# Branch hints, gates in the one-hot rows, and a reordered end in a one-core attention and mixture-of-experts kernel

## Chip, cores and metric

The kernel runs on one core of a Trainium2 chip, as one program in one launch. The metric is the device time in microseconds (us); a kernel's time is the median of its runs.

## What is computed

The reference is two blocks over 256 tokens of width 1024, batch 1. The first is a sparse attention mixer; the second has two layers, each with an attention and convolution mixer, a feed-forward part and a gated side input. The change touches only the end of the last layer: the mixture of 8 experts of which each token uses 2, and the gate behind it.

```python
top_vals, top_idx = lax.top_k(logits, TOP_K)            # TOP_K = 2 of 8 experts
gates = jax.nn.softmax(top_vals, axis=-1)
for e in range(N_EXPERTS):
    out = out + combine[:, e:e + 1] * swiglu(xt, w1[e], w3[e], w2[e])
h = h + out
gate = jax.nn.sigmoid(rmsnorm(h, ple_norm_g[i]) @ ple_gate_w[i])
h = h + gate * (p[i] @ ple_proj_w[i])
```

## The kernel before

All is float32. Tokens stand as two tiles of 128 rows (`NT = 2`, index `t`). The weights, 491 MB of DMA traffic in all, are streamed by SyncE (SP) in pieces of 512 KB into a ring of buffers; a piece's buffer is filled again once its last reader is done. All engines run their instructions in the order in which the code is written (`manual_schedule`).

Experts are run in steps (`STEPS`) of one expert and one chunk of its hidden width, two experts alternating. Only the tokens of an expert are gathered, by a one-hot matrix of token against place in the expert's list: the first 64 places (`SET`) always, the places from 65 to 96 and from 97 to 128 (two times `SUB`) only if the expert has so many tokens. A step has three weight products, each through `wide` (line 1475): w1 and w3 (`up`) and w2 (`down`). `wide` issues the product of the first 64 places and puts off `rest`, a branch on TensorE alone (`If(many() > SET)`, line 1496, with one for over 96 inside, line 1499), which is issued by `catch_up` after the next product's first weight part. There are 98 such outer branches: 96 from 32 steps of three products, and 2 from `result_logits`. Where the count is at most 64, TensorE jumps over the instructions of the rare products.

When an expert is finished, `way_back` (line 1424) builds the one-hot rows `oh2` from positions and the 0/1 selection (`where`, line 1408), TensorE turns them round (`turn`) into `back`, and `scatter` (line 1575) multiplies `back` by the expert's results `ys` into PSUM and adds that to the residual `h`, weighted with the gate, by VectorE's scalar_tensor_tensor (line 1596). `scatter` is called per token tile, in two pieces that lie between other products, with a branch of its own (line 1602).

At the end the last gate matrix (`gate_w`) is multiplied with the expert results directly: `result_T` turns the last expert's results round and `result_logits` (line 1655) multiplies them with `gate_w` into `zs`, which is scattered like `ys`, but into `logit`. The end of `experts` (line 1767 on) is: last `down`, scatter of `ys` into `h` for both tiles with one branch (line 1781), `result_logits`, square sums of `h` on ScalarE (`halves`, line 451) and the root on VectorE (`rstd`), scatter of `zs` into `logit`, and per quarter (one tile, 512 columns) sigmoid on ScalarE (line 1799), product with `value` and sum with `h` on VectorE (lines 1800, 1801) and the store.

Of the kernel before, what the change touches and what calls it, by code (L numbers as in the profile page):

```python
# [19 lines left out]
P = 128  # L20
D = 1024
S = 256
NT = 2
# [190 lines left out]
class _Net:  # L214
# [1190 lines left out]

    def where(self, pos, t, e):
        return pos[:, t, e : e + 1], self.sel[:, t, e : e + 1], ALU.is_equal, ALU.mult

    def places(self, sp, e, base=0):

# [11 lines left out]

    def way_back(self, sp, e, base=0):

        pos = self.based(sp, base)
        oh = self.t(sp, [P, NT, 3, P], "oh2")
        for t in range(NT):
            first = self.slots[:, 0:SET].unsqueeze(1).to_broadcast([P, 2, SET])  # L1430
            self.nc.vector.tensor_scalar(oh[:, t, 0].rearrange("p (d n) -> p d n", d=2), first, *self.where(pos, t, e))
            rest = self.slots[:, SET:CAP].rearrange("p (s n) -> p s n", s=2).unsqueeze(2).to_broadcast([P, 2, 4, SUB])
            self.nc.vector.tensor_scalar(oh[:, t, 1:3].rearrange("p s (d n) -> p s d n", d=4), rest, *self.where(pos, t, e))
# [12 lines left out]
        return back, turn  # L1446
# [29 lines left out]
    def wide(self, key, outs, lhs, n, many, take, mids=None):  # L1476

        mids, ws = mids or {}, self.ws
        parts = ws.take(key)
        end = parts[-1][1][1]

        def product(s, j, k0, k1):
            w = ws.get(j)
            d = 4 if s else 2
            r, m = P // d, 2 * n // d
            c = m if s == 2 else 0
            for k in range(k0, k1):  # L1490
# [81 lines left out]
    def results(self):  # L1572
        return self.t(self.act, [P, 2, 512], "xl", bufs=3)

    def scatter(self, t, e, back, ys, many=None, to=None, tag="tr"):


        ps = []
        to = self.h[:, t, :] if to is None else to[t]
        rows = [slice(SET * j, SET * j + SET) for j in range(2)]  # L1580

        def first():
            ps[:] = [self.bank(tag) for _ in range(2)]
            for j in range(2):
                self.mm(ps[j], back[rows[j], 0, t * P : t * P + P], ys[rows[j], 0, :], start=True, stop=True, skip_group_check=True)

        def others():
            for i in range(2):
                for d in range(2):
                    for j in range(2):  # L1590
                        self.mm(ps[j][:, d * 256 : d * 256 + 256], back[rows[j], 1 + 2 * i + d, t * P : t * P + P],
                                ys[rows[j], 1, i * 256 : i * 256 + 256], start=False, stop=i == 1, skip_group_check=True)

        def add(j):
            v = to[:, j * 512 : j * 512 + 512]
            self.nc.vector.scalar_tensor_tensor(v, ps[j], self.gates[:, t, e : e + 1], v, ALU.mult, ALU.add)  # L1596

        def second():
            if many is None:
                others()  # L1600
            else:
                with self.tc.If(many() > SET):  # L1602
                    others()
            for j in range(2):
                add(j)

        return first, second, others, add

# [77 lines left out]
    def experts(self, sp):  # L1686
# [23 lines left out]
        for i, (e, c) in enumerate(STEPS):  # L1710
# [14 lines left out]
            if done is not None:  # L1725
                back[done], turn = self.way_back(sp, done)
                mids.setdefault(6, []).append(turn)
                late = {2 + 2 * t + k: [f] for t in range(NT) for k, f in enumerate(self.scatter(t, done, back[done], ys[done], F(number, done))[:2])}
            if i == LAST + 2:
                for j, (t, k0) in enumerate((t, k0) for t in range(NT) for k0 in (0, 4)):  # L1730
                    mids.setdefault(3 + j, []).append(F(self.gate_inputs, t, k0))
# [13 lines left out]
                zs = self.t(self.act, [P, 2, 512], "x", bufs=3)  # L1745
            if i == LAST + 7:
                x = STEPS[LAST][0]
                late = {2 * t + k: [f] for t in range(NT) for k, f in enumerate(self.scatter(t, x, back[x], zs, F(number, x), self.logit)[:2])}
# [19 lines left out]
        turn()  # L1768
        self.catch_up()
        hidden(*prev)  # L1770
        finish(*prev[:2])
        self.result_T(ys[e], yT[1], 0)
        self.catch_up()
        self.result_T(ys[e], yT[1], 1)
        self.sets.pop("mm")

        def scattered(ys, to):
            steps = [self.scatter(t, e, back[e], ys, None, to, ("tr", "mm")[t]) for t in range(NT)]
            for f in steps:
                f[0]()  # L1780
            with self.tc.If(many() > SET):
                for f in steps:
                    f[2]()
            return [F(f[3], j) for f in steps for j in range(2)]

        for f in scattered(ys[e], None):
            f()
# [7 lines left out]
        for (t, j), f in zip(((t, j) for t in range(NT) for j in range(2)), scattered(zs, self.logit)):  # L1795
            f()
            c = slice(j * 512, j * 512 + 512)
            sg, hv = self.t(self.wp, [P, 1024], "wl", bufs=PARTS)[:, 0:512], self.h[:, t, c]
            nc.scalar.activation(sg, self.logit[t][:, c], AF.Sigmoid, scale=r[:, t : t + 1])  # L1799
            nc.vector.tensor_mul(sg, sg, self.value[t][:, c])  # L1800
            nc.vector.tensor_add(hv, hv, sg)  # L1801
            nc.sync.dma_start(self.out[:, t, c], hv)

    def overflow(self, sp, xT, ys):
# [4 lines left out]
        with self.tc.If(most > CAP):  # L1809
            self.ws = _Direct(self, self.stream)  # L1810
            for e in range(NE):
                oh = self.places(sp, e, CAP)
                for k in (0, 4):
                    self.gather(oh, xT, k)
                back, turn = self.way_back(sp, e, CAP)
                turn()
                for c in range(NC):
                    n = CHUNKS[c][1] // 2
                    self.up(("w1", e, c), xT, s, n, None, True)
                    self.up(("w3", e, c), xT, s, n, None, False)  # L1820
                    self.down(("w2", e, c), ys, self.hidden(sp, s, n), n, None, c == 0)
                for t in range(NT):
                    for f in self.scatter(t, e, back, ys)[:2]:
                        f()
            self.ws = self.stream

# [237 lines left out]
```

## Time and profile before

| | us |
|---|---|
| median of 3 runs | 1792.64 (1789.38 to 1797.64) |
| the profiled execution's own time | 1791.19 |
| its span, first to last instruction | 1789.0 |
| TensorE (PE) busy | 1670.9 (93%) |
| VectorE (DVE) busy | 670.6 (37%) |
| ScalarE (ACT) busy | 504.8 (28%) |
| GpSimd (POOL) busy | 144.0 (8%) |
| granted TensorE clock, mean | 0.977 |

The profile is of one execution. A row of the timeline names start and length in us, the engine, the line of the kernel, the operation, output and inputs by the program's names, shape, and how many equal instructions were merged; in brackets stands how long the engine was idle before and what released it. "PEq L1496" as a releaser is TensorE's instruction queue at that branch. PEld is TensorE's loading of weights, and a float32 product shows as two matrix instructions. The experts run from about 800 us on; the last weights land just before 1740 us, and what follows is the end.

### The profile page before, as it was taken

To read this page: it belongs to the slowest core of one execution; us is meant where nothing else is said; L and a number is where in the kernel's file an instruction comes from. 1 tells how busy PE (TensorE), PEld (TensorE's weight loads), DVE (VectorE), ACT (ScalarE), POOL (GpSimd) and SP (SyncE) were. 2 spreads that over 40 slices of the span, in tenths; PEclk is the share of its full clock that TensorE was granted. 3 is DMA by queue.
4 is the path that set the end of the run, shared out by engine and by line. 5 is a ranking of instruction groups with operands and counts; after the bars stand their busy time and mean duration, and the time that the engine had idled before them with its cause. 6 is when DMAs were issued, how large, how long until landed. Compare 5 with 4: busy or idle time off the path is not lost. (4 is left out here: it accounts for less than half of the span.)

```text
span 1789.0 us, 24489 instructions
## 1 busy us (share of the span) xinstructions
PE 1670.9 (93%) x9778; PEld 1001.4 (56%) x9781; DVE 670.6 (37%) x1131; ACT 504.8 (28%) x831; POOL 144.0 (8%) x146
## 2 busy tenths in 40 slices
PE   8999989999999989999997999999999989898984
PEld 6887768778888868873324434445333354233331
DVE  6656776585555586651111220011211113101214
ACT  5546645654444456631000000000000000010001
POOL 2002332510000022400000000000000000000000
PEclk9999999999999999999999999999999999999987
DMA  8654335445555558478999998999699998888960
GB/s 275 199 170 145 104 106 191 143 152 188 188 187 181 180 180 307 162 305 344 406 414 410 386 370 337 366 396 403 230 378 401 412 411 323 313 327 320 391 256 25
DMA packets 174777, 491.24 MB, mean 275 GB/s; under 512 B 16670, under 2 KB 21206, under 8 KB 174576
## 3 DMA queue, kind: packets, MB, share of 16 engines
q1 hardware_dynamic: 170224, 474.54, 70.8%
q0 software_dynamic: 4352, 13.74, 2.6%
q8 instruction: 160, 2.62, 0.6%
q14 instruction: 41, 0.34, 0.1%
HBM read 486.08 MB, written 2.14 MB: 273 GB/s over the span
## 5 line engine op out<-in xcount | busy, mean ns | idle before, releaser
L287 PE MATMUL mm<-wh,xh 128*128 128x512 f32 (+3 forms) x888 | 317.4, 433 | 13.1 <-PEq L1809 6.8
L335 DVE TENSOR_TENSOR wl<-raw,wh 128x1024 fp32r<-128x1024 f32 x206 | 260.8, 1276 | 129.6 <-ACT wh L331 120.0
L287 PE MATMUL mm<-wh,xl 128*128 128x512 f32 x680 | 271.2, 399 | 1.0 <-DVE xl L506 0.9
L331 ACT CAST wh<-raw 128x1024 fp32r<-128x1024 f32 x218 | 227.0, 1049 | 128.6 <-PE mm L287 66.6
L287 PE MATMUL mm<-wl,xh 128*128 128x512 f32 (+3 forms) x924 | 253.9, 425 | 2.3 <-PEq L1496 2.0
L1536 DVE TENSOR_TENSOR sw_s<-sw_s,s 128x512 f32<-128x512 f32 (+1 forms) x64 | 39.7, 620 | 414.1 <-PE s L287 377.4
L287 PE MATMUL mm<-raw,xh 128*64 128x512 f32 (+3 forms) x1340 | 185.8, 456 | 8.8 <-PEq L1496 6.7
L287 PE MATMUL o<-raw,sw_g 128*64 128x512 f32 (+1 forms) x1228 | 182.6, 496 | 10.8 <-PEq L1496 8.3
L287 PE MATMUL s<-raw,xh 128*64 128x512 f32 (+3 forms) x1344 | 176.9, 453 | 12.6 <-PEq L1496 9.8
L287 PEld LDWEIGHTS mm<-wh,xh 128*128 128x128 f32 (+2 forms) x888 | 141.2, 176 | 59.9 <-issue 19.2
L287 PEld LDWEIGHTS mm<-wl,xh 128*128 128x128 f32 (+2 forms) x924 | 141.0, 172 | 54.0 <-issue 14.2
L287 PEld LDWEIGHTS mm<-wh,xl 128*128 128x128 f32 x680 | 129.3, 190 | 28.9 <-DVE xl L506 2.6
L1548 ACT COPY sw_g<-tr 128x512 f32<-128x512 f32 (+1 forms) x32 | 17.0, 532 | 440.2 <-PE tr L290 409.9
L287 PEld LDWEIGHTS o<-raw,sw_g 128*64 128x64 f32 (+1 forms) x1228 | 68.4, 124 | 114.7 <-issue 91.9
L287 PEld LDWEIGHTS s<-raw,xh 128*64 128x64 f32 (+1 forms) x1344 | 69.2, 124 | 111.6 <-issue 76.8
L287 PEld LDWEIGHTS mm<-raw,xh 128*64 128x64 f32 (+1 forms) x1340 | 67.7, 125 | 97.3 <-issue 73.7
L1534 ACT ACTIVATE sw_s<-mm 128x512 f32<-128x512 f32 (+1 forms) x64 | 34.8, 544 | 195.7 <-PE mm L287 161.0
L1557 DVE TENSOR_TENSOR xl<-xl,o 128x512 f32<-128x512 f32 x48 | 32.9, 686 | 144.6 <-PE o L287 131.4
L287 PE MATMUL s<-wh,xh 128*64 128x512 f32 (+5 forms) x292 | 62.9, 493 | 5.2 <-PEq L1602 3.8
L287 PE MATMUL o<-wh,sw_g 128*128 128x512 f32 (+2 forms) x264 | 60.9, 478 | 3.5 <-DMA raw<-in_moe_w_dram 2.0
L333 POOL TENSOR_TENSOR wl<-raw,wh 128x1024 fp32r<-128x1024 f32 x12 | 30.3, 2554 | 324.4 <-ACT wh L331 304.4
L287 PE MATMUL o<-wl,sw_g 128*64 128x512 f32 (+2 forms) x224 | 51.9, 515 | 3.6 <-DMA wl<-in_moe_w_dram 1.5
(388 smaller groups left out, 1661.9 us busy)
## 6 DMA issues: line engine op xcount, KB each, us to landing
raw<-in_moe_w_dram SPq DMA_DIRECT2D x465, 512.0 KB, 9.9
wh<-in_moe_w_dram SPq DMA_DIRECT2D x100, 512.0 KB, 9.8
wl<-in_moe_w_dram SPq DMA_DIRECT2D x100, 512.0 KB, 10.0
raw<-in_dense_w_dram SPq DMA_DIRECT2D x84, 512.0 KB, 4.6
raw<-in_w_in_dram SPq DMA_DIRECT2D x48, 512.0 KB, 4.4
raw<-in_nsa_w_in_dram SPq DMA_DIRECT2D x44, 512.0 KB, 5.1
raw<-in_w_o_dram SPq DMA_DIRECT2D x16, 512.0 KB, 4.9
raw<-in_ple_gate_w_dram SPq DMA_DIRECT2D x16, 512.0 KB, 6.3
```

The costliest lines, as they stand in the source:

```text
L287: self.nc.tensor.matmul(out, lhsT, rhs, start=start, stop=stop, **kw)
L331: self.nc.scalar.copy(wh, v)
L333: self.nc.gpsimd.tensor_tensor(wl, v, wh.bitcast(F32), ALU.subtract)
L335: self.owed.append(lambda: self.nc.vector.tensor_sub(wl, v, wh.bitcast(F32)))
L1534: nc.scalar.activation(s[:, i, :n], ps[i][:, :n], AF.Silu)
L1536: nc.vector.tensor_mul(s[:, i, :n], s[:, i, :n], ps[i][:, :n])
L1548: copy(g[:, i, : n // P, :], ps[:, :n].rearrange("p (q n) -> p q n", n=P))
L1557: self.nc.vector.tensor_add(ys[:, i, :], ys[:, i, :], y[i])
```

## The change

1. Each outer branch of `wide` gets a label, and halfway through the parts of its product the code marks "LikelyTaken" for that label on TensorE.
2. `where` takes the values it multiplies with; `way_back` passes the gates in place of the 0/1 selection. So `back` holds the gate, and the sum in `scatter` becomes a plain tensor_add.
3. At the end, `logit` is copied into four PSUM banks by a product with the identity, ahead of the last `down`; the scatter of `zs` is added up on top of it there, and the sigmoid reads PSUM.
4. The scatter of `ys` into `h` is done per tile with a branch each; square sums and root stand ahead of `result_logits`. A sigmoid of one column loads ScalarE's table early.
5. Both copies of `result_logits` are on ScalarE. The four sigmoids are issued first, then the products on VectorE; two of the four sums with `h` are on GpSimd.

```diff
-    def where(self, pos, t, e):
-        return pos[:, t, e : e + 1], self.sel[:, t, e : e + 1], ALU.is_equal, ALU.mult
+    def where(self, pos, t, e, value=None):
+        return pos[:, t, e : e + 1], (self.sel if value is None else value)[:, t, e : e + 1], ALU.is_equal, ALU.mult
...
-            self.nc.vector.tensor_scalar(oh[:, t, 0].rearrange("p (d n) -> p d n", d=2), first, *self.where(pos, t, e))
+            self.nc.vector.tensor_scalar(oh[:, t, 0].rearrange("p (d n) -> p d n", d=2), first, *self.where(pos, t, e, self.gates))
...
+        self.n += 1
+        label = f"rare_{self.n}"
+
         def rest():
-            with self.tc.If(many() > SET):
+            with self.tc.If(many() > SET, label=label):
...
+            if i == len(parts) // 2 and many is not None:
+
+                self.tc.mark_branch_hint_location(label, "LikelyTaken", engines=(mybir.EngineType.PE,))
...
-            self.nc.vector.scalar_tensor_tensor(v, ps[j], self.gates[:, t, e : e + 1], v, ALU.mult, ALU.add)
...
+                self.nc.vector.tensor_add(v, v, ps[j])
...
+    def spread(self, ps, t, back, ys, start):
+        for j in range(2):
+            r = slice(SET * j, SET * j + SET)
+            self.mm(ps[j], back[r, 0, t * P : t * P + P], ys[r, 0, :], start=start, stop=True, skip_group_check=True)
...
         def take(i):
-            if i:
-                self.nc.vector.tensor_copy(zs[:, i, :], z[i])
-            else:
-                self.nc.scalar.copy(zs[:, i, :], z[i])
+            self.nc.scalar.copy(zs[:, i, :], z[i])
...
         hidden(*prev)
+        nc.scalar.activation(self.t(self.act, [P, 1], "warm"), self.gT[:, 0:1], AF.Sigmoid)
+
+        lg = []
+        for t, tag in zip(range(NT), ("mm", "s")):
+            self.sets.pop(tag)
+            lg.append([self.bank(tag) for _ in range(2)])
+            for j in range(2):
+                self.mm(lg[t][j], self.ident, self.logit[t][:, j * 512 : j * 512 + 512], start=True, stop=True)
         finish(*prev[:2])
...
-        self.result_logits(yT[1], zs, many)
+        for t in range(NT):
+            for f in self.scatter(t, back[e], ys[e], many):
+                f()
         sq = self.sq_tile(NT)
         junk = self.t(self.wp, [P, 1024], "wh", bufs=PARTS)
         for t in range(NT):
             self.halves(sq[:, t], t, junk)
         r = self.rstd(sq)
+        self.result_logits(yT[1], zs, many)
         self.catch_up()
...
+        for t in range(NT):
+            self.spread(lg[t], t, back[e], zs, False)
+        with self.tc.If(many() > SET):
+            for t in range(NT):
+                self.spread_rare(lg[t], t, back[e], zs)
...
+        for t, _, ps, sg in pieces:
+            nc.scalar.activation(sg, ps, AF.Sigmoid, scale=r[:, t : t + 1])
+        for i, (t, c, _, sg) in enumerate(pieces):
+            hv = self.h[:, t, c]
             nc.vector.tensor_mul(sg, sg, self.value[t][:, c])
-            nc.vector.tensor_add(hv, hv, sg)
+            (nc.vector if i > 1 else nc.gpsimd).tensor_tensor(hv, hv, sg, ALU.add)
             nc.sync.dma_start(self.out[:, t, c], hv)
```

The order of the instructions in the built program shows where these land. First the start of TensorE's program, in the change:

```order
L2059 UNCONDITIONAL_BRANCH
L2059 BRANCH_PREFETCH_HINT x98
L290 MATMUL tr_132<-c_ident_86,h_85 128x128 x4
L290 MATMUL s_137<-c_ident_86,x_89 128x8
L290 MATMUL tr_154<-c_ident_86,h_85 128x128 x4
```

Before, the first transposes follow the branch directly. All 98 hints stand here, ahead of the first work, in the reverse order of their branches; none stands in the products, where the code marks them.

Second, TensorE between the turning of the last hidden values (`sw_s`) and the last `down` (`o<-raw,sw_g`), in the change:

```order
L290 MATMUL tr_27053<-c_ident_86,sw_s_26641 128x128 x2
L287 MATMUL mm_27059<-x_24962,c_ident_86 128x512
L287 MATMUL mm_27060<-x_24962,c_ident_86 128x512
L287 MATMUL s_27063<-x_24963,c_ident_86 128x512
L287 MATMUL s_27064<-x_24963,c_ident_86 128x512
L287 MATMUL o_7225<-raw_26830,sw_g_27048 64x512 x2
L287 MATMUL o_7225<-raw_26832,sw_g_27048 64x512 x2
L287 MATMUL o_7225<-raw_26834,sw_g_27048 64x512 x2
L287 MATMUL o_7225<-raw_26836,sw_g_27048 64x512 x2
```

The four products with the identity (`c_ident`; the `x` tiles are `logit`) are new; before, the `down` follows the transposes at once.

Third, the last work of VectorE (`wl` holds the sigmoids, `raw` the `value` tiles), in the change:

```order
L1809 TENSOR_TENSOR wl_27281<-wl_27281,raw_14224 128x512
L1809 TENSOR_TENSOR wl_27282<-wl_27282,raw_14224 128x512
L1809 TENSOR_TENSOR wl_27283<-wl_27283,raw_14308 128x512
L1810 TENSOR_TENSOR h_85<-h_85,wl_27283 128x512
L1809 TENSOR_TENSOR wl_27284<-wl_27284,raw_14308 128x512
L1810 TENSOR_TENSOR h_85<-h_85,wl_27284 128x512
```

Before, 13 instructions stand there: a copy of `zs` and four times scatter's sum, product and sum. The sums of `wl_27281` and `wl_27282` with `h` are now GpSimd's last two instructions.

## Rows read from the trace of the kernel before

**Rows 1.** The page: busy time of the engines; DMA share in 40 slices.
```profile
PE 1670.9 (93%) x9778; PEld 1001.4 (56%) x9781; DVE 670.6 (37%) x1131; ACT 504.8 (28%) x831; POOL 144.0 (8%) x146
...
DMA  8654335445555558478999998999699998888960
```

**Rows 2.** Stretches of the experts: length, busy time by engine, clock, DMA share, GB/s.
```profile
800.00:1000.00 200.00, 177.89 (x896) 73.38 (x900) 26.93 (x55) 19.41 (x35) 0.00 (x0) 0.97 0.98 390
1000.00:1200.00 200.00, 197.70 (x1768) 82.76 (x1769) 28.57 (x45) 11.72 (x20) 0.00 (x0) 1.00 0.93 366
```

**Rows 3.** TensorE's waits at branches: us in total, times, longest.
```profile
PE o L287 <- PEq L1496: 12.7, 16, 3.0
PE s L287 <- PEq L1496: 11.5, 21, 5.4
PE mm L287 <- PEq L1496: 10.7, 12, 2.9
...
PE s L287 <- PEq L1602: 5.1, 12, 3.3
```

**Rows 4.** Instructions of TensorE's queue at lines 1496 and 1781: ns min/median/max.
```profile
L1496 PEldq COMPARE_BRANCH  x98: 65/417/7128, 807.6 to 1764.2; - x98
...
L1781 PEldq COMPARE_BRANCH  x2: 219/219/219, 1756.3 to 1769.3; - x2
L1781 PEldq EVENT_SEMAPHORE  x2: 51/51/51, 1760.0 to 1771.4; - x2
```

**Rows 5.** Timeline of the first 20 us: ScalarE's start, first work of TensorE, ScalarE's wait.
```profile
0.73 1.28 ACT L633 ACT_TABLE_LOAD   x1 [0.73 <-PEq L2059]
...
4.48 1.09 PE L290 MATMUL tr<-c_ident,h 128*128 128x128 f32 x4 [4.48 <-DMA h<-in_x_dram]
...
15.45 1.04 ACT L331 CAST wh<-raw 128x1024 fp32r<-128x1024 f32 x1 [2.66 <-DMA raw<-in_nsa_w_in_dram]
```

**Rows 6.** The page: DMA queue of instruction blocks: packets, MB, share of 16 engines.
```profile
q8 instruction: 160, 2.62, 0.6%
```

**Rows 7.** Groups by shape: products on all 128 rows with 512 columns.
```profile
L287 PE MATMUL tr<-raw,xh 128*128 128x512 f32 x32 | 14.3, 599 | 0.0
```

**Rows 8.** Timeline of the end, TensorE.
```profile
1748.17 3.65 PE L287 MATMUL o<-raw,sw_g 128*64 128x512 f32 x16
...
1755.23 2.20 PE L287 MATMUL tr<-xl,back 64*128 64x512 f32 x3
...
1757.26 2.73 PE L287 MATMUL mm<-xl,back 64*128 64x512 f32 x3
1760.14 8.48 PE L287 MATMUL o<-raw,xl 128*64 128x512 f32 x32
...
1770.26 1.02 PE L287 MATMUL mm<-x,back 64*128 64x512 f32 x4
```

**Rows 9.** Stretches of the end, columns as in rows 2.
```profile
1755.00:1760.00 5.00, 4.99 (x11) 1.56 (x9) 0.76 (x2) 0.00 (x0) 0.00 (x0) 0.62 0.00 0
1760.00:1765.00 5.00, 4.86 (x16) 1.73 (x18) 2.73 (x4) 0.00 (x0) 0.00 (x0) 0.70 0.02 3
```

**Rows 10.** Timeline of the end, ScalarE and VectorE.
```profile
1768.66 0.58 ACT L1660 COPY x<-o 128x512 f32<-128x512 f32 x1 [20.91 <-PE o L287]
...
1773.76 0.69 DVE L1658 COPY x<-o 128x512 f32<-128x512 f32 x1
1775.14 0.72 ACT L1799 ACTIVATE wl<-x,rms_y 128x512 f32<-128x512 f32 x1 [2.15 <-DVE x L1596]
...
1785.22 0.69 DVE L1801 TENSOR_TENSOR h<-h,wl 128x512 f32<-128x512 f32 x1
```

**Rows 11.** Timeline at 655 to 668 us: VectorE alone, then beside GpSimd.
```profile
655.79 0.69 DVE L1395 TENSOR_TENSOR h<-h,x 128x512 f32<-128x512 f32 x1
...
661.35 5.15 POOL L333 TENSOR_TENSOR wl<-raw,wh 128x1024 fp32r<-128x1024 f32 x2 [19.95 <-PE mm L287]
...
664.34 2.71 DVE L1395 TENSOR_TENSOR h<-h,x 128x512 f32<-128x512 f32 x1
```

More of the change, by code (lines that the diff above doesn't have):

```diff
@@ L1430, in way_back @@
             first = self.slots[:, 0:SET].unsqueeze(1).to_broadcast([P, 2, SET])
-            self.nc.vector.tensor_scalar(oh[:, t, 0].rearrange("p (d n) -> p d n", d=2), first, *self.where(pos, t, e))
+            self.nc.vector.tensor_scalar(oh[:, t, 0].rearrange("p (d n) -> p d n", d=2), first, *self.where(pos, t, e, self.gates))
             rest = self.slots[:, SET:CAP].rearrange("p (s n) -> p s n", s=2).unsqueeze(2).to_broadcast([P, 2, 4, SUB])
-            self.nc.vector.tensor_scalar(oh[:, t, 1:3].rearrange("p s (d n) -> p s d n", d=4), rest, *self.where(pos, t, e))
+            self.nc.vector.tensor_scalar(oh[:, t, 1:3].rearrange("p s (d n) -> p s d n", d=4), rest, *self.where(pos, t, e, self.gates))
         back = self.t(sp, [P, 5, S], "back")
@@ L1573, in results, with scatter @@
         return self.t(self.act, [P, 2, 512], "xl", bufs=3)
-    def scatter(self, t, e, back, ys, many=None, to=None, tag="tr"):
+    def scatter(self, t, back, ys, many=None, to=None):
         ps = []
         to = self.h[:, t, :] if to is None else to[t]
-        rows = [slice(SET * j, SET * j + SET) for j in range(2)]
         def first():
[L1583 to L1595, printed above, removed]
-            self.nc.vector.scalar_tensor_tensor(v, ps[j], self.gates[:, t, e : e + 1], v, ALU.mult, ALU.add)
+            ps[:] = [self.bank("tr") for _ in range(2)]
+            self.spread(ps, t, back, ys, True)
@@ L1598, in second @@
         def second():
             if many is None:
-                others()
+                self.spread_rare(ps, t, back, ys)
             else:
                 with self.tc.If(many() > SET):
-                    others()
+                    self.spread_rare(ps, t, back, ys)
             for j in range(2):
-                add(j)
-        return first, second, others, add
+                v = to[:, j * 512 : j * 512 + 512]
+                self.nc.vector.tensor_add(v, v, ps[j])
+        return first, second
@@ new lines, in spread, with spread_rare @@
+    def spread(self, ps, t, back, ys, start):
+        for j in range(2):
+            r = slice(SET * j, SET * j + SET)
+            self.mm(ps[j], back[r, 0, t * P : t * P + P], ys[r, 0, :], start=start, stop=True, skip_group_check=True)
+    def spread_rare(self, ps, t, back, ys):
+        for i in range(2):
+            for d in range(2):
+                for j in range(2):
+                    r = slice(SET * j, SET * j + SET)
+                    self.mm(ps[j][:, d * 256 : d * 256 + 256], back[r, 1 + 2 * i + d, t * P : t * P + P],
+                            ys[r, 1, i * 256 : i * 256 + 256], start=False, stop=i == 1, skip_group_check=True)
@@ L1727, in experts @@
                 mids.setdefault(6, []).append(turn)
-                late = {2 + 2 * t + k: [f] for t in range(NT) for k, f in enumerate(self.scatter(t, done, back[done], ys[done], F(number, done))[:2])}
+                late = {2 + 2 * t + k: [f] for t in range(NT) for k, f in enumerate(self.scatter(t, back[done], ys[done], F(number, done)))}
             if i == LAST + 2:
@@ L1747, in experts @@
                 x = STEPS[LAST][0]
-                late = {2 * t + k: [f] for t in range(NT) for k, f in enumerate(self.scatter(t, x, back[x], zs, F(number, x), self.logit)[:2])}
+                late = {2 * t + k: [f] for t in range(NT) for k, f in enumerate(self.scatter(t, back[x], zs, F(number, x), self.logit))}
             if n < 512:
@@ L1770, in experts @@
         hidden(*prev)
+        nc.scalar.activation(self.t(self.act, [P, 1], "warm"), self.gT[:, 0:1], AF.Sigmoid)
[3 more added lines that the diff above has]
+            lg.append([self.bank(tag) for _ in range(2)])
+            for j in range(2):
+                self.mm(lg[t][j], self.ident, self.logit[t][:, j * 512 : j * 512 + 512], start=True, stop=True)
         finish(*prev[:2])
@@ L1774, in experts @@
         self.result_T(ys[e], yT[1], 1)
[L1775 to L1787, printed above, removed]
-        self.result_logits(yT[1], zs, many)
+        for t in range(NT):
+            for f in self.scatter(t, back[e], ys[e], many):
+                f()
         sq = self.sq_tile(NT)
@@ L1793, in experts @@
         r = self.rstd(sq)
+        self.result_logits(yT[1], zs, many)
         self.catch_up()
[L1795 to L1799, printed above, removed]
+        for t in range(NT):
[3 more added lines that the diff above has]
+                self.spread_rare(lg[t], t, back[e], zs)
+        pieces = [(t, slice(j * 512, j * 512 + 512), lg[t][j], self.t(self.wp, [P, 1024], "wl", bufs=PARTS)[:, 0:512])
+                  for t in range(NT) for j in range(2)]
+        for t, _, ps, sg in pieces:
+            nc.scalar.activation(sg, ps, AF.Sigmoid, scale=r[:, t : t + 1])
+        for i, (t, c, _, sg) in enumerate(pieces):
+            hv = self.h[:, t, c]
             nc.vector.tensor_mul(sg, sg, self.value[t][:, c])
-            nc.vector.tensor_add(hv, hv, sg)
+            (nc.vector if i > 1 else nc.gpsimd).tensor_tensor(hv, hv, sg, ALU.add)
             nc.sync.dma_start(self.out[:, t, c], hv)
@@ L1822, in overflow @@
                 for t in range(NT):
-                    for f in self.scatter(t, e, back, ys)[:2]:
+                    for f in self.scatter(t, back, ys):
                         f()
```

## Prediction

> **What bounds the kernel now.** I read the page first: TensorE is busy 93% of the span, no other engine over 37% [rows 1]. So it is TensorE's own time, and what stops it, that counts. The DMA line of the page shows the second bound: from the nineteenth slice on, where the experts run, most digits are 8 or 9 [rows 1]. Then I read the experts' stretches. From 800 to 1000 us the DMA share is 0.98 and TensorE works 177.89 of 200 us; from 1000 to 1200 us, where rare products run, TensorE works 197.70 of 200 us [rows 2]. The experts change from one limit to the other, so a microsecond saved on TensorE before 1000 us may be eaten by late weights.
>
> TensorE's waits come next. Its own queue at the outer branches makes it wait 12.7 + 11.5 + 10.7 = 34.9 us in 49 waits, at the scatter's branches 5.1 us more [rows 3]. The queue shows why: the 98 branches of line 1496 took from 0.065 to 7.128 us, a jump inside the scatter at the end 0.219 us [rows 4]. Some jumps land on instructions that are not there yet. Most of that time never reaches the array, since the queue runs ahead of it.
>
> Last comes the end. After the weights are in, everything hangs on one chain: last product, scatter, gate product (8.48 us), copy, norm, scatter, and four quarters one after the other, from 1768.66 to 1785.91 us [rows 8, 10].
>
> **The change, part by part.** *Hints.* The order of the built program puts all 98 ahead of TensorE's first transpose, none near its branch. So I count no gain at the branches; the only cost is at the start. Engines are released at 0.73 us, and TensorE begins at 4.48 us, when the first tokens have landed [rows 5]: 3.75 us are free. No row shows a hint. The nearest are what this queue alone handles: 0.051 us for a semaphore instruction, 0.065 for the shortest branch, 0.219 for a jump [rows 4]. I take the first, since a hint neither compares nor jumps: 98 x 0.051 = 5.0 us, 1.3 us over the cover. ScalarE, which feeds TensorE there, waits 2.66 us for weights at 15.45 us [rows 5], and most of the delay goes there. I take +0.5; below, 0; above, 98 x 0.219 = 21.5, which less 3.75 and 2.66 is +15.
>
> The hints also move all later code, so other jumps will find their target missing. The waits at branches are 40 us in all; which way they move cannot be read, so I take 0 and one eighth, 5 us, to both sides.
>
> *Gates in the rows back.* The one-hot instructions keep their shape. The sum loses its factor and nothing else, on an engine that is busy 37% of the span [rows 1]: 0.
>
> *Identity products.* Four products of 128 rows by 512 columns, new, in TensorE's order between the last transposes and the last `down` (1748.17 us [rows 8]). All weights are there, so nothing hides them. Sixteen such products (32 instructions) took 14.3 us [rows 7], 0.9 each: +3.6. What waits behind them is the whole chain of the end.
>
> *Scatter into `h`.* Before, four products for both tiles from 1755.23 to 1759.99, then the gate product at 1760.14 [rows 8]: 4.9 us. Now the second tile waits for its PSUM banks until the first tile's two sums are read: 2.0 (1755.23 to 1757.26) + 1.4 for two sums of 0.69 [rows 10] + 2.0 for the second tile: 5.4. So +0.5.
>
> *After the gate product.* Before: 1768.63 to 1785.91, 17.3 us. Now norm and root lie beside the gate product; they took the 5.1 us from the copy to 1773.76 [rows 10] and have 8.48 us of cover. If that went, up to 5 us come back. What is left: copy 0.6 (1768.66), scatter of four products 2.0 (from the copy's end at 1769.24 to 1771.28 [rows 8, 10]), branch 0.2, first sigmoid 0.72, together 3.5; the other sigmoids run beside VectorE. Then VectorE has four products and two sums at 0.69, 4.1 us. GpSimd's two sums: a sum of 1024 columns takes 5.15 / 2 = 2.6 us there, one of 512 then 1.2 to 1.3, so 2.5 us.
>
> These do not run beside each other. VectorE's sum of 128x512 takes 0.69 us alone and 2.71 us beside GpSimd's [rows 11]: it stood still while GpSimd worked. So I add them: 4.1 + 2.5 = 6.6, and the stretch is 3.5 + 6.6 = 10.1 against 17.3, -7.2. With both at full speed it would be 2.5 us less. The Trainium skill (SBUF — State Buffer, "SBUF: two separate sides") says that a VectorE operation with two SBUF inputs and a GpSimd operation that reads SBUF hold their shared ports exclusively for the whole instruction. By that rule the two sums on GpSimd are no gain, and VectorE alone, with 8 x 0.69 = 5.5 us, would end earlier; the trace agrees with 2.71 against 0.69 us. No row shows a GpSimd sum of this width.
>
> *Copies and table.* The second copy of `zs` on ScalarE (0.58) is behind the first, and nothing of the first 64 places waits for it; the table load lies where ScalarE is idle. Both 0.
>
> **Sum:** +0.5 + 3.6 + 0.5 - 7.2 = -2.6 us. On the profiled execution's 1791.19 us that is 1788.6. That execution is 1.45 us below the median of the runs, 1792.64, so I forecast a median of **1790 us**.
>
> The clock is the term I cannot place: from 1755 to 1765 us the granted clock is 0.62 and 0.70 [rows 9], partly at 1.2 instead of 2.4 GHz, after TensorE had stood idle between short transposes. That costs 0.76 x 5 / 2 + 0.60 x 5 / 2 = 3.4 us. The identity products keep TensorE busy just before, the split scatter makes a new gap; I leave it as it is, 3.4 us to either side. My forecast's own range is 1783 to 1798.
>
> **The rivals.** *A, the forecast:* 0.63.
>
> *B, the hints act although they stand at the start.* Then 49 waits fall from 34.9 us to about 0.22 each: 24 us. For it: the branches really cost that. Against it: 98 of them stand in one place, some 800 us ahead of the first branch, and before 1000 us the DMA share of 0.98 would take part of it. 12 to 24 us less than the forecast: 1778 to 1766. 0.15. The Trainium skill (Runtime: NRT & Kernel Launch, "Instruction fetch mechanics") calls prefetch purely sequential, with a taken jump out of the fetched pages waiting for a fetch. By that B gains nothing and the forecast stands; the trace agrees with branches of up to 7.128 us, and shows no hint.
>
> *C, slower: each hint at the start fetches its target.* The instruction blocks took 0.6% of 16 engines' span for 160 packets: 0.006 x 16 x 1789 / 160 = 1.07 us each [rows 6]. If TensorE's queue stood still for each, that is 105 us, less 6.4 of cover: 1888 us. It decides from about 0.19 us a hint (18.5 us, less 6.4, against the 3.1 the end gains, is +9). Against it: nothing in the first 20 us needs a jump's target. 0.10.
>
> *D, the end gains more:* GpSimd beside VectorE costs nothing and the clock stays up, -2.5 and -3.4: 1784 us. Rows 11 speak against its first half. 0.12.
>
> **How the numbers follow.** A measurement of this kernel tells about 0.5% from no change, 9 us: faster means under 1783.7, slower over 1801.6. Faster: B's 0.15, a third of D, and 0.03 of A: 0.22. Slower: C's 0.10 and 0.01 of A: 0.11. Same: 0.67. The range that leaves out half of B and all of C, 1774 to 1802, holds 0.8.
>
> **What would show it.** Right: TensorE's first transpose at 5.5 to 7 us instead of 4.48; waits at the outer branches still about 35 us; the four identity products as 3.6 us ahead of the last `down`; root before the gate product's end; VectorE's products at up to 2 us each beside GpSimd's sums; and 33 to 36 us from the last `down`'s old place to the last sum, where it was 37.7. Wrong: waits at branches under 15 us (B), first work after 20 us (C), or VectorE at 0.69 us throughout the end (D).

## The result, and the profile after

The changed kernel takes **1808.64 us** (median of 8 runs, 1803.7 to 1827.93). The kernel before took 1787.03 us beside it (8 runs). The ratio is 1.0131, with a 95% interval from 1.0088 to 1.0174: slower by about 21 us, 1.3%. The prediction had 1790 us and a range of 1774 to 1802.

The profiled execution spans 1801.9 us, 12.9 more than before. It is the fastest of the eight, 4.9 us under their median, and the profiled one of before took 1791.19 us, 4.2 more than the median beside it; so the profiles show a smaller loss than the medians. Three marks on TensorE's queue tell where: the first outer branch, the 96th, and the end. Before, they lie at 807.6, 1746.2 and 1789.0 us; after, at 803.1, 1758.9 and 1801.9 us. So the stretch to the first branch is 4.5 us shorter, the **experts' stretch** from first to 96th branch 17.3 us longer (955.8 for 938.5), and the rest 0.2 us longer. In these two executions the whole loss is in the experts.

TensorE's queue, first the hints, then the outer branches (ns min/median/max, first and last start in us):

```profile
L2059 PEldq BRANCH_PREFETCH_HINT  x98: 31/31/52, 0.8 to 9.8; - x98
```

```profile
L1500 PEldq COMPARE_BRANCH  x98: 65/414/7183, 803.1 to 1784.1; - x98
```

A hint is shown with 31 ns, but 98 of them fill 9.0 us, one every 0.092 us. The timeline of TensorE's start shows what stood behind them:

```profile
9.96 1.09 PE L290 MATMUL tr<-c_ident,h 128*128 128x128 f32 x4 [9.96 <-issue]
```

It was 4.48 us before, with the tokens as releaser [rows 5]; now it is TensorE's own queue. The median and the longest of the branches are about what they were [rows 4], but their sum is not (167.9 us for 136.7), nor are the waits they cause. TensorE's waits (us in total, times, longest):

```profile
PE o L287 <- PEq L1500: 20.3, 17, 3.5
PE tr L290 <- PEq L1500: 14.3, 5, 5.2
PE mm L287 <- PEq L1818: 11.5, 1, 11.5
...
PE mm L287 <- PEq L1500: 6.8, 9, 2.5
PE s L287 <- PEq L1500: 6.1, 20, 3.0
...
PE s L287 <- PEq L1596: 2.3, 12, 0.6
```

The rows of L1500 sum to 47.5 us in 51 waits, where rows 3 have 34.9 in 49. At the jump over the overflow (code for experts with more than 128 tokens, not entered here), L1818, TensorE waits 11.5 us; before it was this:

```profile
PE mm L287 <- PEq L1809: 6.8, 1, 6.8
```

Together that is 12.6 us more at the outer branches and 4.7 more at the overflow, with 2.8 less at the scatter's branches (L1596; rows 3 have 5.1): 14.5 of the 17.3 us.

The end of the program, timeline of TensorE, ScalarE, VectorE and GpSimd (start, length):

```profile
1761.12 2.89 PE L287 MATMUL mm<-x,c_ident 128*128 128x512 f32 x4
...
1763.84 1.88 PE L287 MATMUL s<-x,c_ident 128*128 128x512 f32 x4
...
1765.65 3.65 PE L287 MATMUL o<-raw,sw_g 128*64 128x512 f32 x16
...
1772.71 3.05 PE L287 MATMUL tr<-xl,back 64*128 64x512 f32 x4
...
1776.64 2.67 PE L287 MATMUL tr<-xl,back 64*128 64x512 f32 x4 [0.87 <-DVE h L1600]
...
1779.45 9.13 PE L287 MATMUL o<-raw,xl 128*64 128x512 f32 x32
...
1783.55 0.16 DVE L447 SCALAR_TENSOR_TENSOR rms_y<-rms_z,rms_y 128x2 f32<-128x2 f32 x1
...
1788.62 1.07 ACT L1665 COPY x<-o 128x512 f32<-128x512 f32 x2 [7.08 <-PE o L287]
...
1792.11 2.96 DVE L1809 TENSOR_TENSOR wl<-wl,raw 128x512 f32<-128x512 f32 x3 [8.40 <-ACT wl L1806]
...
1792.96 3.24 POOL L1810 TENSOR_TENSOR h<-h,wl 128x512 f32<-128x512 f32 x2 [1049.84 <-DVE wl L1809]
...
1795.11 1.63 DVE L1810 TENSOR_TENSOR h<-h,wl 128x512 f32<-128x512 f32 x1
...
1797.38 0.69 DVE L1810 TENSOR_TENSOR h<-h,wl 128x512 f32<-128x512 f32 x1
```

Here the change does much of what it was made for: the norm's root is ready at 1783.7 us, 4.9 us ahead of the gate product's end, and from there to the last sum it takes 9.5 us instead of 17.3 [rows 8, 10]. Ahead of that it pays: identity products (logit times the identity matrix, into PSUM) 4.5 us (1761.12 to 1765.65), and 6.7 us instead of 4.9 from the first scatter to the gate product, which itself takes 9.13 us for 8.48. From the last `down`'s old place to the last sum it is 37.0 us, where it was 37.7.

### The profile page after: what moved, and what is told of

Same layout as the page of the kernel before. It is cut to its first block, busy times and chain, and to the rows that moved or that the text cites. A ratio compares the mean times of both kernels' runs of the same rounds, so it can differ in the third digit from the quotient of the medians.

```text
span 1801.9 us, 24603 instructions
## 1 busy us (share of the span) xinstructions
PE 1667.1 (93%) x9786; PEld 1005.8 (56%) x9789; DVE 665.0 (37%) x1123; ACT 505.9 (28%) x834; POOL 147.3 (8%) x148
## 5 line engine op out<-in xcount | busy, mean ns | idle before, releaser
L287 PE MATMUL mm<-wh,xh 128*128 128x512 f32 (+3 forms) x888 | 317.7, 435 | 16.4 <-PEq L1818 11.5
L287 PE MATMUL s<-raw,xh 128*64 128x512 f32 (+3 forms) x1344 | 177.9, 455 | 10.1 <-PEq L1500 5.2
## 6 DMA issues: line engine op xcount, KB each, us to landing
raw<-in_moe_w_dram SPq DMA_DIRECT2D x465, 512.0 KB, 10.1
```

The source lines that it names most:

```text
L287: self.nc.tensor.matmul(out, lhsT, rhs, start=start, stop=stop, **kw)
```

## The experiments

Four theories stood at the start. **T1:** the 98 hints move all later TensorE code by 98 places, and other jumps find their target missing. **T2:** the hints disturb the fetching of code by what they make the queue do. **T3:** the 9 us at the start are the loss. **T4:** the loss comes from the rest of the change. A place is the room of one instruction in the program; the head is where TensorE's program starts. In the table stand the median, the ratio to the runs of before beside it with its interval, and from the profiled execution TensorE's first product, the first outer branch, and the stretch from the first to the 96th (all us; e11 has no such branch at six of the experts). Three columns come from one execution each.

| kernel | median | ratio | first product | first branch | experts' stretch |
|---|---|---|---|---|---|
| before | 1787 | | 4.5 | 807.6 | 938.5 |
| after | 1808.6 | 1.0131 [1.0088, 1.0174] | 10.0 | 803.1 | 955.8 |
| e1 after, no hints | 1782.2 | 0.9977 [0.9958, 0.9996] | 4.9 | 800.9 | 938.0 |
| e2 before, hints | 1812.9 | 1.0151 [1.0127, 1.0176] | 10.0 | 811.0 | 953.7 |
| e3 before, aligned head | 1808.5 | 1.0118 [1.0087, 1.0149] | 4.9 | 808.3 | 954.4 |
| e4 before, hints, aligned | 1792.7 | 1.0037 [1.0019, 1.0055] | 10.4 | 810.9 | 935.6 |
| e5 before, 98 fillers | 1798.9 | 1.0063 [1.0043, 1.0084] | 8.1 | 817.1 | 936.5 |
| e6 after, 158 fillers | 1798.4 | 1.0070 [1.0044, 1.0096] | 21.8 | 811.5 | 930.2 |
| e7 before, 128 fillers | 1813.5 | 1.0138 [1.0099, 1.0177] | 10.3 | 814.4 | 953.4 |
| e8 hints in place | 1785.9 | 1.0002 [0.9981, 1.0023] | 4.6 | 797.6 | 942.5 |
| e9 more code jumped over | 1903.4 | 1.0671 [1.0627, 1.0716] | 4.2 | 795.4 | 1061.2 |
| e10 less code jumped over | 1730.3 | 0.9684 [0.9656, 0.9712] | 4.4 | 797.6 | 890.0 |
| e11 no unused branches | 1708.2 | 0.9549 [0.9524, 0.9575] | 4.0 | | |
| e12 sums on VectorE | 1780.8 | 0.9959 [0.9933, 0.9985] | 4.5 | 802.8 | 939.2 |
| e13 one rare body | 1750.1 | 0.9775 [0.9737, 0.9813] | 4.3 | 799.0 | 911.6 |
| e14 hints with less code | 1737.6 | 0.9704 [0.9665, 0.9743] | 10.0 | 803.0 | 892.2 |

### Hints alone, all but hints, and an aligned head

e1, the change without its hints:

```diff
-            if i == len(parts) // 2 and many is not None:
-                self.tc.mark_branch_hint_location(label, "LikelyTaken", engines=(mybir.EngineType.PE,))
```

> The change with the hints alone taken out. Three theories put the lost time on the hints: T1, they move all later code of TensorE by 98 places, so that other jumps find their target missing; T2, the hints themselves disturb the fetching of instructions during the experts; T3, the 9 us that they take at the start. A rival, T4, puts it on the rest of the change (scatter per tile, identity products, sums on GpSimd). T1, T2 and T3 expect 0.99 to 1.00 of the time before, T4 expects 1.008 to 1.015. The end, from the last down's place to VectorE's last sum, should stay at 37 us as in the change.

e2, the kernel before with these lines and the label of the branch added, and nothing else of the change:

> The kernel before with the 98 hints alone added, all at the head of TensorE's program. T1, T2 and T3 expect 1.008 to 1.018 of the time before; T4 expects 1.00. T3 expects the first branch of the experts some 5 us later than before, T1 and T2 expect the loss between the first branch and the overflow's branch.

e3 and e4, the kernel before and that of e2 with one line at the head of the program:

```diff
+        nc.tensor.addr_align(256, offset=0, max_nops=0)
```

> The kernel before, its TensorE program moved so that its first work starts on a boundary of an instruction block (256 places); the padding is jumped over. A reference for the next run, and a first sample of what the place of the code alone does. T1 expects anything from 0.99 to 1.015 of before; T2, T3 and T4 expect 1.00 within 0.004.

> The kernel before with the 98 hints at the head and the same boundary behind them, so that every branch and target lies in its block as in the run with the boundary alone. T1 expects the same time as that run within 0.5%, T2 expects 1% more than that run, T3 expects 5 to 9 us more than that run, all of it before the first branch of the experts.

Without the hints the change is faster than before by 0.2%; with nothing but the hints, before is slower by 1.5%. So T4 falls, and taking out or adding the hints takes away or brings the whole loss. But e3 loses as much in the experts with no hint in it (954.4), and e4 loses nothing there with all 98 (935.6): T2 does not hold as it stands, and T3 is too small, since e4 has the same late start as the change. Which branches are long is fixed by the head of the program: the 98 durations of before and e1 agree with a correlation of 0.99, those of after and e2 with 0.99, before and after with 0.09. What e3 and e4 have in common, the same place of the code, did not give them the same pattern (0.17), nor the same time, as T1 expected. That they share it shows in the packets that bring TensorE's code: in both the seventh starts after 1508 of its products and weight loads, the eighth after 1786.

### The place of the code, by fillers

e5, e6 and e7 put 98, 158 and 128 empty TensorE instructions at the head: e5 and e7 of before, e6 of the whole change.

```diff
+        for k in range(98):
+            nc.tensor.nop(hint="pad", nofuse=True)
```

> The kernel before with 98 empty TensorE instructions at the head, no hint: all later TensorE code lies 98 places further on, as in the kernel with the 98 hints alone (1812.9 us). If the place of the code alone loses the time, 1805 to 1816 us, from the first outer branch to the 78th 763 to 770 us as with the hints (763.9) and not 750.3, and the same of the 98 outer branches are the long ones as with the hints alone (correlation of their durations over 0.9). If it takes hints to lose it, 1786 to 1793 and 750 us. The third view, that the change's loss comes from PE standing 9 us at the start, expects the start's share alone, 0 to +5 us.

> The whole change, hints and all, with 158 empty TensorE instructions at the head besides, so that the code behind lies 98 + 158 = 256 places further on than in the change without its hints, which is one whole block of 16384 bytes at 64 bytes a place. If what counts is where the code lies within its blocks, the pattern of long branches is that of the change without hints (correlation over 0.9), the stretch from first to 78th outer branch is 752.7 +- 3 us and the time 1782 plus what the longer start costs: 1783 to 1795. If the hints cost by themselves or the loss has to do with something other than the place in a block, 1803 to 1825 us. If it is a place in something larger than a block, neither pattern comes back and the time can be anywhere from 1782 to 1815.

> The kernel before with 128 empty TensorE instructions at the head: half a block. By the theory of the place this is another draw: a third pattern (correlation under 0.6 with those of before and of 98 places) and a time anywhere between 1783 and 1815 us, with the stretch from first to 78th outer branch carrying the difference (750 to 770). By the theory that the place is without effect, 1786 to 1793.

e7 is a third head with a long experts' stretch, again without a hint. Its pattern was to agree to less than 0.6 with before and with 98 places: it does with before (0.06) and e5 (0.48), but with e2 and after it agrees to 0.78, though their code lies 30 places apart. e6 brings the experts' stretch back (930.2, and to the 78th branch 751.1, in the expected 752.7 ± 3), though its pattern agrees with e1's only to 0.64, and its time, 1798.4, is above the expected 1795; the profiled execution is the fastest of its seven, 9.6 us under that median. e5 missed: to the 78th branch it took 758.5 (expected 763 to 770), its pattern agrees with e2's to 0.59 (expected over 0.9), and over the whole experts' stretch it lost nothing (936.5); of the 9.8 us by which its profile is longer than that of before, 9.5 lie ahead of the first branch. So the same places, once with hints and once with fillers, gave 953.7 and 936.5 us. T1 in its strict form, that place alone fixes the loss, falls too. What the eleven kernels with bodies of this size show (before, after, e1 to e8, e12) is two groups of experts' stretches, 930 to 943 and 953 to 956 us; neither hints nor place nor start alone separates them.

### Hints in place

e8 holds each hint in the code, halfway through the product that its branch belongs to:

```diff
             if i == len(parts) // 2 and many is not None:
+                with self.tc.block():
+                    self.tc.mark_branch_hint_location(label, "LikelyTaken", engines=(mybir.EngineType.PE,))
+                    product(0, j, k0, k1)
```

> The change with each of its 98 hints standing inside the code, about 80 instructions ahead of the branch it names, instead of all at the head (a block of code of its own holds it there, which adds an empty branch or two on each engine). If a hint makes the TensorE queue fetch the target ahead, the long branches go: of 98 outer ones under 8 over 0.7 us, waits at the outer branches 5 to 15 us in place of 35 to 48, the stretch from first to 78th branch 725 to 740 us and the time 1755 to 1772. If a hint does nothing but take its own 0.09 us, there remain some 16 to 24 long branches, the waits stay 35 to 50 us and the time is 1782 to 1812, by the place the code then has. If a hint fetches, but the fetch throws out what runs next, the waits grow over 60 us and the time over 1820.

The queue's rows of e8:

```profile
L2061 PEldq BRANCH_PREFETCH_HINT  x98: 31/35/51, 791.7 to 1761.0; - x98
```

```profile
L1500 PEldq COMPARE_BRANCH  x98: 74/442/7354, 797.6 to 1764.1; - x98
```

34 branches are over 0.7 us (before had 35, not the 16 to 24 that I named), the longest 7.354 us: even here the hints take no wait away. They ran 0.2 to 9.8 us ahead of their branches (median 2.8). Also where the hint ran 4.3 to 5.0 us ahead, three branches took 6.0 to 6.3 us, and the packet with their code started only 3.5 to 3.8 us after the branch. So the hint did not ask for it.

### The amount of code

What the queue waits for can be read from the instruction packets. In all traces with outer branches every one over 0.7 us, 450 of 450, ends 1.33 to 1.55 us after a packet of 16384 bytes on the instruction queue (q8) has landed, and all were jumps; a branch whose body runs was never long. Ahead of the experts, before fetches 30 such packets for 7827 TensorE instructions, so one for about 256 places, or 64 bytes each. I call that a block. A product's code is mostly 332 places, of which 264 are the bodies that are jumped over, so 1.30 blocks. Before, a block came every 7.4 us on average in the experts (126 in 938 us, median gap 6.5), and a quarter of the gaps was under 5.8 us.

The packets also give the price of a single jump. Of the 450, 136 end with a packet that starts 3.3 to 3.9 us after the branch; the packet takes 1.0 us and the branch goes on 1.4 us after it, 6.05 us in all (median). In 15 of the 136 the DMA share (from 2 us ahead of the branch to its end) was 0.5 to 0.95, in the others more; the 15 took 6.1 us too. So the wait is the time from the branch to a block that had not been fetched yet, and these runs don't show that the weights' transfers make it long.

e9 adds a third body, never entered; e10 leaves out the inner body at the experts that don't enter it; e11 leaves out both bodies and the branch at the six experts that enter neither. e10 and e11 are right only for inputs with these counts.

```diff
                 with self.tc.If(many() > SET + SUB):
...
+                with self.tc.If(many() > CAP + SET):
+                    for j, (k0, k1, _, _) in parts:
+                        product(2, j, k0, k1)
```

```diff
-                with self.tc.If(many() > SET + SUB):
+                if key[1] == 1:
+                    with self.tc.If(many() > SET + SUB):
```

```diff
-            with self.tc.If(many() > SET, label=label):
+            if key[1] in (1, 2):
+                with self.tc.If(many() > SET, label=label):
```

> The change without its hints, with a third body (the products of the last 32 slots once more, for counts over 192, which never runs here) in each of the 98 outer branches: a branch that isn't entered then jumps over 398 places of code in place of 264. By the theory that a long branch is a wait for code, which is fetched block by block whether it runs or is jumped over, a product passes 466 places, 1.82 blocks in place of 1.30; at the 5.8 to 6.2 us between the closest fetches that is 10.6 to 11.3 us a product against some 9.7 now: the stretch from first to 78th outer branch 810 to 880 us, the sum of the outer branches 220 to 400 us in place of 141, the instruction blocks about 160 + 51, and the time 1840 to 1960. By the theory that only the place counts and not the amount, another draw: 1780 to 1815, the sum 130 to 170.

> The change without its hints, and without the inner body (the products of the last 32 slots) at the seven experts that do not enter it with these inputs and at the gate product; expert 1, which enters it, keeps it, so the work done is the same. A jump is 134 places in place of 264, a product passes 0.8 block in place of 1.3, some 4.6 us of fetches against 9.7. If the waits at the branches are waits for blocks that the fetches bring late: under 12 long ones (over 0.7 us) in place of 33, their sum under 70 us in place of 141, about 45 blocks fewer, TensorE's idle time at the outer branches under 15 us in place of 35, and 1782 becomes 1748 to 1768. If something else than the amount of code sets them, 20 to 36 long ones and 1775 to 1810.

> The change without its hints, and without outer bodies and their branches at the six experts that do not enter them with these inputs (and at the gate product): what all 74 jumps together are worth. Code then runs on in a straight line. If TensorE's waits at the branches are on the path that sets the end, these 35 to 45 us go, with the jumps' own 0.2 to 0.4 us each: 1740 to 1760 us. If the weights' transfers would set the pace without them, the time stops nearer 1765 to 1778, with TensorE waiting for raw instead.

The outer branches of e9, and the instruction queue on its page:

```profile
L1500 PEldq COMPARE_BRANCH  x98: 65/3380/7475, 795.4 to 1883.7; - x98
```

```profile
q8 instruction: 208, 3.41, 0.7%
```

The same of e10 (its 110 rows are the 98 branches and 12 jumps at the end of bodies that ran), then TensorE's waits there:

```profile
L1500 PEldq COMPARE_BRANCH  x110: 65/217/2725, 797.6 to 1710.1; - x110
```

```profile
q8 instruction: 118, 1.93, 0.5%
```

```profile
PE s L287 <- PEq L1500: 2.9, 18, 0.2
PE o L287 <- DMA raw<-in_moe_w_dram: 2.6, 13, 0.3
...
PE o L287 <- PEq L1500: 2.1, 13, 0.2
...
PE mm L287 <- PEq L1500: 1.6, 10, 0.2
```

Code that is never run costs its fetch: with more of it the median branch rises from e1's 0.418 to 3.380 us and the time by 121 us on e1; with less, 33 long branches become 2 and the time falls by 52 us. That is more than the 31.1 us for which e1's array stood idle at these branches. The stretches show more (length, busy TensorE, its weight loads, VectorE, ScalarE, GpSimd, granted clock, DMA share, GB/s); first e1, then e10:

```profile
800.00:1000.00 200.00, 177.06 (x905) 71.25 (x908) 27.00 (x47) 18.93 (x33) 0.00 (x0) 0.97 1.00 392
1000.00:1200.00 200.00, 197.42 (x1798) 84.01 (x1794) 27.31 (x43) 11.63 (x20) 0.00 (x0) 1.00 0.95 368
```

```profile
800.00:1000.00 200.00, 187.62 (x1012) 70.75 (x1011) 29.70 (x51) 17.18 (x32) 0.00 (x0) 1.00 1.02 401
1000.00:1200.00 200.00, 198.26 (x1936) 88.50 (x1934) 25.60 (x41) 11.42 (x20) 0.00 (x0) 1.00 0.99 388
```

Between 800 and 1000 us TensorE works 10.6 us more in e10, weights come a little faster (401 GB/s against 392), and the granted clock is 1.00 of its 2.4 GHz instead of 0.97. From the first branch to the end TensorE is idle 47.1 us in e10 and 85.4 in e1, of that 7 and 31 at the outer branches; and the same work takes it 883.1 instead of 894.2 us, at a mean granted clock of 0.99 instead of 0.97. These two make up the 49.4 us by which that part is shorter. e10 was expected at 1748 to 1768 us and e11 at 1740 to 1760; both came out faster, for I had counted the waits at the branches alone. e11, with no jump left at six experts, is 74 us under e1; 87 blocks are fetched.

e14 is e10 with the hints back at the head:

> The whole change with its 98 hints at the head, with the inner bodies left out at the experts that don't enter them, as in e10 (1730.3 us without hints). If the hints lose time by where they put later code, and that matters only because fetches have no time to spare, then here no more than the later start is left: +3 to +8 us on e10, 1733 to 1739, under 8 long branches. If the hints cost by themselves (by what they make the queue fetch, or later at the branches they name), the 26 us between the change with and without them come back: 1748 to 1765.

It came out as T1 and the late blocks had it: 4 long branches, and 7.3 us on e10 instead of the 26.4 between after and e1. In the two profiled executions 5.4 us lie ahead of the first branch and 2.2 in the experts. So what the hints cost beyond the start hangs on long jumps that pass much code.

### A version for use, and the sums

e13 makes one body of the two, laid out as the first 64 rows; it needs nothing left out:

```diff
-                for h in range(d):
-                    self.mm(outs[s > 0][r * h : r * h + r, c : c + m], lhs(s, k), w[:, k - k0, h * m : h * m + m],
-                            start=k == 0 and s < 2, stop=k == end - 1, skip_group_check=s > 0)
+                for h in range(2):
+                    self.mm(outs[s][SET * h : SET * h + SET, 0:n], lhs(s, k), w[:, k - k0, h * n : h * n + n],
+                            start=k == 0, stop=k == end - 1, skip_group_check=s > 0)
...
-                with self.tc.If(many() > SET + SUB):
-                    for j, (k0, k1, _, _) in parts:
-                        product(2, j, k0, k1)
```

> The change without its hints, with the two bodies for 32 slots each (264 places jumped over) made one body for all 64 further slots, laid out as the first 64 are: 66 places of code, nothing left out. A product passes some 135 places, 0.53 block, 3.2 us of fetches. By the theory of late blocks: no more than 3 long branches, their sum under 40 us, some 80 blocks in the experts fewer. Against that stands more matrix work at expert 2, which ran one body (3.7 us a product) and now runs one of twice that (7.8 us by the 64-row rows): 12 times 4.1 = 49 us at most, 0 to 10 us at expert 1. So 1708 to 1730 (little of the work exposed, as in e10) up to 1785 (all of it); I take 1755.

It beats both kernels: 1750.07 us, 2.25% under before (interval 1.87 to 2.63%). No branch is over 0.7 us. The 20 us above e10 are added matrix work, within the 49 us that were named as the most: from the first branch on TensorE is busy 905.9 us in e13 and 883.1 in e10, 22.8 more, and idle 47.4 and 47.1.

e12 has the four last sums on VectorE:

> The change without its hints, with all four of the last sums on VectorE instead of two on GpSimd. The prediction took 2.5 us as the price of the two engines' keeping one another off. If GpSimd's two sums (1.6 us each) delay VectorE's work beside them as the trace suggests (three products 2.96 us in place of 3 x 0.69 and one sum 1.63), the stretch behind the gate product is 0.3 to 1.0 us shorter than 9.5 us; if GpSimd takes real work off VectorE, it is 0.5 to 1.5 us longer. The whole time is expected within 4 us of 1782 either way.

From the copies to the last sum it took 8.9 us (1770.49 to 1779.38), where the change takes 9.5, and e1, from which e12 differs in these sums alone, 9.4 (1767.24 to 1776.68): 0.6 us shorter, as expected of engines that hinder each other. The whole time does not resolve it.

## Why the prediction was wrong

**The step that failed** is "The hints also move all later code ... which way they move cannot be read, so I take 0 and one eighth, 5 us, to both sides." It named the right place, and the direction could not be read from the profile; the size was wrong. The term was 0 with 5 us to either side, and the experts' stretch grew by 17.3 us. Heads moved without a hint drew 936.5 (e5), 953.4 (e7) and 954.4 us (e3) for the experts, against 938.5 before. I had sized it by the idle time of the array at the branches [rows 3]. The row that would have warned was there: 160 packets [rows 6] are about what 98 products of 332 places (127 blocks) and the code ahead of them (30) need if the jumped-over bodies are fetched too. That is a block every 7.4 us in the experts, where one jump to a block not yet fetched costs 6; e9, e10 and e14 show how much hangs on it. That the loss by the hints hangs on this is shown by e14; why 98 hints bring it and 98 fillers at the same places don't stays open.

**The start** was predicted at +0.5 us from 0.051 us a hint. Measured: 0.092 us each, first product 5.5 us later. The cover that was to take it, ScalarE's wait of 2.66 us [rows 5], took only about 1: ScalarE's copy at line 826 starts at 29.92 us in after and at 25.82 before, at 30.31 in e14 and at 25.79 in e10, 4.1 and 4.5 us later. What is left of it at the experts can't be read from one execution: without hints at the head or fillers, the first branch lies anywhere between 795 and 808 us, so after's own 803.1 says nothing.

**The gates in the rows back** at 0 fit: e1's experts' stretch is before's (938.0 and 938.5).

**The end** was predicted at -3.1 us (3.6 + 0.5 - 7.2) and shows -0.8 in the one profile: identity products 4.5 for 3.6 (+0.9), the gate product begins 1.8 us later instead of 0.5 (+1.3) and takes 0.65 us more, while the last stretch is 0.6 better (9.5 for 10.1). Part of that is the clock, which the sum left as it was: the identity products ran at a granted clock of 0.78 in after, and in e1, at 1.00, they took 3.5 us (1740.84 to 1744.37), the term of the forecast; the gate product ran at 0.77 where before it had 0.83. In e1 the way from the last `down`'s old place to the last sum is 35.8 us (1740.84 to 1776.68), within the 33 to 36 of the forecast. By the runs, all of the change but the hints gives 4.3 us (e1, interval 0.7 to 7.5). The Trainium skill's rule on the shared ports (SBUF — State Buffer, "SBUF: two separate sides") is borne out in sign: three VectorE products take 2.96 us instead of 2.07 beside GpSimd's sums, and VectorE alone is 0.6 us faster. GpSimd's sums cost VectorE 1.8 of the 2.5 us that I added: its six last operations took 6.0 us (1792.11 to 1798.07), where six times 0.69 is 4.1.

**The rivals.** B falls: at the head the waits grew, and even in place the hints remove none (e8). C had the sign and neither mechanism nor size: a hint costs 0.09 us, not a fetch, and the loss is 800 us later. The Trainium skill (Runtime: NRT & Kernel Launch, "Instruction fetch mechanics") calls prefetch sequential and a jump out of the fetched pages a stall; the block counts 208 (e9), 162 (after), 118 (e10) and 87 (e11) and waits of up to 7.5 us (e9) agree. The Trainium skill also says there that fetching is otherwise hidden behind the pace of dispatch; the waits counted here are all at jumps, so no run decides on that.

**Left open:** what puts one head in the group with the long stretches and another in the other. 98 hints and 98 fillers at the same places differ by 17 us in the experts, and e3 and e4 share their places and not their pattern. The start of the first product does not separate the groups either: it is 10.0 us in after and e2, 10.3 in e7 and 4.9 in e3, all long, and 10.4 in e4, not long. A difference of some microseconds in when fetches and weights meet may do it; that was not tried.

## What to carry to other kernels

Count the code that a jump passes over, not only the time of the branch: here each 256 places of TensorE's code cost a fetch, whether they run or not, a jump to code not yet fetched cost about 6 us, and rare bodies written into the stream can set the pace (74 us of 1782 here). Before blaming or praising an edit that adds or moves instructions on a queue with many taken branches, run the same program with some empty instructions at its head: here that alone, or an aligned head, is worth up to 1.4% (e7; e3 1.2%). Make the rare path short before hinting it.

## What the runs showed of the hardware that was not expected

- A branch prefetch hint is shown with 31 ns and holds TensorE's queue for 0.092 us; neither at the head nor in place, 2.8 us (median) ahead of its branch, did it shorten the jumps (34 long ones of 98 in both, up to 7.183 and 7.354 us).
- Instruction blocks of 16384 bytes take 1.0 to 1.1 us in the packet (medians), and a jump whose block is missing goes on 1.33 to 1.55 us after the packet's end (450 cases). Where the packet starts only after the branch, 3.3 to 3.9 us after it, the jump took 6.05 us (median of 136), at a DMA share of 0.5 to 0.95 as at one near 1.
- Eleven kernels with the same experts gave two groups of stretches, 930 to 943 and 953 to 956 us, one execution of each; which jumps are late is fixed by the head (correlation 0.98 to 0.99 between kernels that share one).
